# Second merge gate of a hybrid layer: seven block products in place of eight, with x's block sums kept in DRAM

## The chip, the cores and the metric

One Trainium2 chip, one of its cores. The metric is device time in microseconds for one call of the whole layer, as the median over runs. The engines are TensorE (PE in the profile, its weight loads PEld), VectorE (DVE), ScalarE (ACT), GpSimd (POOL) and SyncE (SP), which here only issues DMAs. Each engine works through its own instructions strictly in the order in which they were written into its queue.

## The reference, cut to what matters

One layer on 512 tokens of width 1024, in float32: gated linear attention (GLA), forgetting attention (FoX), a merge of the two by gates, an output projection, then a gated MLP.

```python
h = rmsnorm(x, norm_mix_g)
gq, gk, gv, gr, glr, fq, fk, fv, ff, g_gla, g_fox = jnp.split(h @ w_in, IN_OFFSETS, axis=-1)
o_gla = ...                       # GLA, then norm and silu(gr)
o_fox = ...                       # FoX attention
y = jax.nn.sigmoid(g_gla + gate_b[0]) * (o_gla @ w_gla_branch) \
    + jax.nn.sigmoid(g_fox + gate_b[1]) * (o_fox @ w_fox_branch)
x = x + y @ w_out
a, val = jnp.split(rmsnorm(x, norm_ffn_g) @ w_up, 2, axis=-1)
...
```

The change concerns `g_fox`, the second gate: a product of h (512 x 1024) with a weight of 1024 x 1024.

## The kernel before, in words

**Splits.** Every weight comes from DRAM as a *piece* of 128 x 1024 floats (512 KB). To keep float32 accuracy a piece is split into a high half `wh` (a cast on ACT, L292) and a low half `wl` (raw minus high, on DVE, L293), and `mm3` (L326) issues three matmuls for one product: high by high, high by low, low by high. `wh` and `wl` have three buffers each (NW = 3), so the split of a piece can only begin when PE is done with the piece three places earlier. The raw pieces sit in places named `raw`, `rawz`, `zr`, with two buffers each. A list, `recipes`, fixes the order of the pieces; `behind(n, ...)` hangs loads and adds onto the split of piece n.

**Seven for eight.** Several products are already done in blocks by Strassen's scheme in Winograd's form: the operands are cut into 2 x 2 blocks, sums of blocks are multiplied, and seven block products (numbered 1 to 7) give the four result blocks. The sums of weight blocks are made by DMA: an accumulating transfer on GpSimd's queue adds a block from DRAM onto a raw piece that lies in SBUF. An "add" (L300) does so in place, once the piece has been split and is no longer wanted; a "sum" (`dma_behind`, L306, issued at L310) does so ahead, behind a one-column copy named `tick`. K of FoX, V of FoX, the output projection and both MLP products work like this, and their products with shared pieces stand several pieces apart. `wsum` are sums of blocks of the last weight, made in DRAM in the same way and spread over the kernel by the tables COPY_AT and ADD_AT.

**The stage around the change.** After the attention (whose last matmuls are at L1041) the kernel runs a loop over `c` from -2 to 7 (L1141). One pass makes one tile of the second gate, `gate_tile` (L926: 24 matmuls of 128 x 512, evicted at L933), two passes ahead of its use, and then the two branch products for the 128 features of c (24 matmuls of 128 x 512), two sigmoids (L1127), and the products of gates and branches (L1156, L1157, L1160), whose results are split again for the output projection (L1119, L1120). At the head of this stage ACT and DVE also make the second operand of the branches: `zr` times its sigmoid `sg` on GpSimd (L1132), times `ogr` on DVE (L1133), split to `ogh` (ACT, L1136) and `ogl` (DVE, L1138).

**x's block sums.** In the GLA stage `pair_sums` and `pair_split` (L724, L726) make four sums of blocks of x, split into halves, for FoX's K and V. Their buffers are given up before the attention.

Of the kernel before, what the change touches and what calls it, by code (L numbers as in the profile page):

```python
# [92 lines left out]
def hybrid_kernel(ctx: ExitStack, tc, xT, xt, wp, wu, wd, wf, wn, pp, aw2, fing, out):  # L93
# [232 lines left out]
    def mm3(ps, ah, al, bh, bl, start, stop, **k):  # L326
        mm(ps, lhsT=ah, rhs=bh, start=start, stop=False, **k)  # L327
        mm(ps, lhsT=ah, rhs=bl, start=False, stop=False, **k)  # L328
        mm(ps, lhsT=al, rhs=bh, start=False, stop=stop, **k)  # L329

# [383 lines left out]
    def pair_split(p, after, tag, tag_low=None):  # L714

        hi = gpool.tile([P, K2, H], F32R, tag=tag, name="h" + tag)
        if tag_low is not None:
            lo = gpool.tile([P, K2, H], F32R, tag=tag_low, name="l" + tag_low)
        else:
            if not lows_left:  # L720
                lows = gpool.tile([P, K2, T], F32R, tag="x2", name="lx2")
                lows_left.extend(lows[:, :, i * H : (i + 1) * H] for i in range(2))
            lo = lows_left.pop()
        nc.scalar.copy(out=hi, in_=sources[p])  # L724
        with tc.issue_after(after.ins):
            nc.vector.tensor_sub(out=lo, in0=sources[p], in1=hi.bitcast(F32))  # L726
# [402 lines left out]
    for h in range(GH):  # L1129
# [8 lines left out]
        nc.vector.tensor_sub(out=ogl[h], in0=zr[h], in1=ogh[h].bitcast(F32))  # L1138
# [581 lines left out]
def _layout(inputs):  # L1720
# [21 lines left out]
    for c in range(-GAHEAD, KD):
        if c + GAHEAD < KD:
            ps.append(by_feature(cols("gf", D), c + GAHEAD))
        if c < 0:
            continue
# [69 lines left out]
```

## Time and profile before

| | us |
|---|---|
| median of 3 runs (689.93 to 690.96) | 690.02 |
| the profiled execution | 689.94 |
| its span, first to last instruction | 688.2 |
| PE busy | 681.4 (99%) |
| DVE busy | 547.8 (80%) |
| ACT busy | 431.5 (63%) |
| POOL busy | 135.5 (20%) |

A group's busy time is the union of its instructions' time; a matmul's duration is longer than its share of the array, since matmuls overlap. So the time of a run of matmuls is read from start to start. Rows of the timeline give start, duration, engine, line, operation, output and inputs, and how often. "[2.43 <-POOL zr L1132]" at a row's end says that the engine sat idle for 2.43 us before it and that the instruction on line 1132 ended this.

### The profile page before, as it was taken

Reading aid. Unit: us, or ns where it says so; the run is one execution under the profiler, and the core shown is the slowest. Engines: PE = TensorE matmul, PEld = TensorE weight load, DVE = VectorE, ACT = ScalarE, POOL = GpSimd, SP = SyncE. Lnnn points to the kernel's source line nnn. Section 1 sums busy time; section 2 is a strip of 40 time slices with the busy share of each in tenths; the row PEclk is TensorE's granted clock in tenths of the full one; section 3 lists DMA queues with packets and bytes.
Section 4 is the critical chain, followed back from the end, with each engine's and each line's share of the span. In section 5 each row is a group of like instructions: output and inputs, shape, how many; then the busy total and the mean of one; then the engine's idle time right before and its main releaser. Section 6 shows DMA issues by size and latency. Waiting matters only on the chain.

```text
span 688.2 us, 10637 instructions
## 1 busy us (share of the span) xinstructions
PE 681.4 (99%) x3875; PEld 585.0 (85%) x3875; DVE 547.8 (80%) x856; ACT 431.5 (63%) x698; POOL 135.5 (20%) x196
## 2 busy tenths in 40 slices
PE   9999999999999999999999999999999999999996
PEld 6788888888888888888888999999999999888885
DVE  6774988858776766687689999888899879977884
ACT  7487675677777744344584965665666666655663
POOL 1125110122321424331110112121122111000222
PEclk9999999999999999999999999999999999999999
DMA  8769488998665489968974898999899888865643
GB/s 313 269 190 317 87 274 218 302 218 207 174 150 122 112 248 196 278 152 212 235 235 126 160 221 198 223 225 218 191 215 216 200 202 261 265 203 173 197 139 122
DMA packets 46184, 142.23 MB, mean 207 GB/s; under 512 B 5396, under 2 KB 9388, under 8 KB 46004
## 3 DMA queue, kind: packets, MB, share of 16 engines
q1 hardware_dynamic: 31156, 92.98, 39.8%
q0 software_dynamic: 11808, 43.52, 35.6%
q10 hardware_dynamic: 3168, 5.05, 2.1%
q8 instruction: 30, 0.49, 0.3%
q14 instruction: 22, 0.18, 0.1%
HBM read 137.32 MB, written 27.28 MB: 239 GB/s over the span
## 4 chain that ended last, share of the span: by engine, by line
PE 99%; DVE 1%; issue 0%; ACT 0%; DVEq 0%; ACTq 0%
PE ps_mm L327 20%; PE ps_mm L329 20%; PE ps_mm L328 20%; PE ps_wide L1462 9%; PE ps_wide L327 5%; PE ps_wide L329 5%; PE ps_wide L328 5%; PE ps_wide L1463 4%; PE ps_lg L1041 1%; PE ps_lg L982 1%; PE ps_pt L1016 1%; PE ps_mm L489 1%; PE ps_ax L327 1%; PE ps_ax L328 1%; PE ps_ax L329 1%; PE ps_ax L377 1%
## 5 line engine op out<-in xcount | busy, mean ns | idle before, releaser
L292 ACT CAST wh<-rawx 128x1024 fp32r<-128x1024 f32 x75 | 76.2, 1016 | 57.3 <-PE ps_mm L328 18.1
L327 PE MATMUL ps_mm<-xw,wh 128*128 128x512 f32 (+1 forms) x320 | 109.3, 341 | 0.0
L328 PE MATMUL ps_mm<-xw,wh 128*128 128x512 f32 (+1 forms) x320 | 107.8, 337 | 0.0
L329 PE MATMUL ps_mm<-xw,wl 128*128 128x512 f32 (+1 forms) x320 | 107.7, 337 | 0.0
L293 DVE TENSOR_TENSOR wl<-rawx,wh 128x1024 fp32r<-128x1024 f32 x75 | 88.3, 1178 | 12.4 <-ACT wh L292 11.4
L293 DVE TENSOR_TENSOR wl<-raw,wh 128x1024 fp32r<-128x1024 f32 x58 | 74.6, 1287 | 14.1 <-ACT wh L292 13.9
L292 ACT CAST wh<-raw 128x1024 fp32r<-128x1024 f32 x58 | 60.7, 1049 | 36.0 <-PE ps_mm L328 18.7
L1462 PE MATMUL ps_wide<-xo,wh 128*128 128x512 f32 x192 | 68.6, 399 | 0.0
L327 PEld LDWEIGHTS ps_mm<-xw,wh 128*128 128x128 f32 x320 | 60.5, 189 | 8.3 <-issue 0.9
L329 PEld LDWEIGHTS ps_mm<-xw,wl 128*128 128x128 f32 x320 | 60.5, 189 | 6.6 <-DVE wl L293 0.2
L328 PEld LDWEIGHTS ps_mm<-xw,wh 128*128 128x128 f32 x320 | 60.6, 189 | 5.9 <-DVE xw L1251 0.2
L1463 PE MATMUL ps_wide<-xo,wl 128*128 128x256 f32 x192 | 54.1, 282 | 0.1
L293 DVE TENSOR_TENSOR wl<-rawz,wh 128x1024 fp32r<-128x1024 f32 x31 | 39.2, 1266 | 16.8 <-ACT wh L292 16.6
L300 POOL DMA_DIRECT2D rawx<-in_wu_dram x30 | 26.3, 877 | 115.7 <-DVE wl L293 77.0
L327 PE MATMUL ps_mm<-xc,wh 128*128 128x256 f32 (+1 forms) x136 | 45.0, 331 | 0.0
L328 PE MATMUL ps_mm<-xc,wh 128*128 128x256 f32 (+1 forms) x136 | 44.6, 328 | 0.0
L329 PE MATMUL ps_mm<-xc,wl 128*128 128x256 f32 (+1 forms) x136 | 44.5, 327 | 0.0
L1462 PEld LDWEIGHTS ps_wide<-xo,wh 128*128 128x128 f32 x192 | 36.1, 188 | 8.2
L292 ACT CAST wh<-rawz 128x1024 fp32r<-128x1024 f32 x31 | 32.4, 1045 | 13.6 <-issue 5.0
L327 PE MATMUL ps_mm<-wh,xw 128*128 128x512 f32 x96 | 37.7, 393 | 0.0
L328 PE MATMUL ps_mm<-wl,xw 128*128 128x512 f32 x96 | 37.4, 390 | 0.0
L329 PE MATMUL ps_mm<-wh,xw 128*128 128x512 f32 x96 | 37.4, 389 | 0.0
(492 smaller groups left out, 1796.0 us busy)
## 6 DMA issues: line engine op xcount, KB each, us to landing
rawx<-in_wu_dram POOLq DMA_DIRECT2D x40, 512.0 KB, 6.9
rawz<-in_wp_dram SPq DMA_DIRECT2D x30, 512.0 KB, 5.0
raw<-in_wp_dram SPq DMA_DIRECT2D x22, 512.0 KB, 5.1
wsum<-in_wd_dram SPq DMA_DIRECT2D x20, 512.0 KB, 6.2
rawx<-in_wu_dram SPq DMA_DIRECT2D x20, 512.0 KB, 5.0
raw<-in_wu_dram SPq DMA_DIRECT2D x20, 512.0 KB, 5.1
rawx<-wsum SPq DMA_DIRECT2D x12, 512.0 KB, 3.7
wsum<-in_wd_dram POOLq DMA_DIRECT2D x10, 512.0 KB, 8.6
```

What stands on the lines that cost most here:

```text
L292: nc.scalar.copy(out=hi[:, :m], in_=raw[:, :m])
L293: nc.vector.tensor_sub(out=lo[:, :m], in0=raw[:, :m], in1=hi[:, :m].bitcast(F32))
L300: nc.gpsimd.dma_start(raw, recipes[i][0], accum_op=ALU.add)
L327: mm(ps, lhsT=ah, rhs=bh, start=start, stop=False, **k)
L328: mm(ps, lhsT=ah, rhs=bl, start=False, stop=False, **k)
L329: mm(ps, lhsT=al, rhs=bh, start=False, stop=stop, **k)
L377: mm(warm, lhsT=nc.const_aps.tensor(1.0, (P, P), BF16), rhs=nc.const_aps.tensor(1.0, (P, T), BF16), start=True, stop=True,)
L489: mm(first[i], lhsT=w[:, i * P : (i + 1) * P], rhs=x, start=(k == j == 0), stop=False)
L982: last = mm(lg[:, place_of_q(qb)], lhsT=a[r, q], rhs=b[r, :n], start=(j == 0), stop=(j == 2))
L1016: nc.tensor.transpose(pt[:, i * P : (i + 1) * P], pr[:, c : c + P], ident)
L1462: mm(ps[:, i], lhsT=wh[:, c], rhs=both[p][:, k], start=first and k == 0, stop=False, skip_group_check=True)
L1463: mm(ps[:, i, 0], lhsT=wl[:, c], rhs=both[p][:, k, 0], start=False, stop=k == KH - 1, skip_group_check=True,)
```

## The change

The second gate's eight tiles become two groups of seven block products. A block product takes one piece, and has 2 x 4 x 3 = 24 matmuls of 256 columns in place of 24 of 512. Group 0 runs ahead of all branch tiles; group 1's first product stands between branches 0 and 1, its other six between branches 1 and 2. Within a group the order is 1, 5, 2, 3, 6, 7, 4. One bank of PSUM takes products 1 and 2, one takes 5 and then 3 on top, and a third starts from a copy of product 1 and takes 6, 7 and 4 on top, so that this bank is read out between 6 and 7 and between 7 and 4, and the copies of 1 and 5 are taken before 2 and 3 go on top.

The four sums of blocks of x, high and low halves, are written to DRAM tiles `again` in the GLA stage (8 transfers of 512 KB on SP's queue) and read back when the attention's buffers are free (8 more on the same queue). Six pieces more are split than before (14 for 8). Block sums of the weight are made by one sum and three adds per group: 6 out of 5, 7 out of 3, 4 out of 6. Of the 24 adds of `wsum`, 16 in place of 10 now hang on the splits of the twelve pieces ahead of the second gate, and 8 in place of 14 on later ones.

```diff
-GAHEAD = 2
-ADD_AT = [32 + i if i < 10 else 42 + (i - 10) * 20 // 14 for i in range(24)]
+ADD_AT = [32 + i if i < 4 else 36 + (i - 4) // 2 if i < 16 else 50 + (i - 16) * 4 for i in range(24)]
+GATE_ORDER = (1, 5, 2, 3, 6, 7, 4)
+GATE_PLACE = {(0, 1): "rawz", (0, 5): "rawz", (0, 2): "raw", (0, 3): "raw"}
+GATE_PLACE.update({(1, 1): "raw", (1, 5): "zr", (1, 2): "rawz", (1, 3): "zr"})
+def branch_order():
+    order = [(0, p) for p in GATE_ORDER] + [0, (1, GATE_ORDER[0]), 1] + [(1, p) for p in GATE_ORDER[1:]]
+    return order + list(range(2, KD))
...
+            g, p = what
+            g11, g12, g21, g22 = (wps[n_gate + 2 * q + g] for q in range(4))
+            new, before = {
+                1: (g11, None), 2: (g21, None), 3: (g22, None), 7: (g12, 3), 5: (g12, None), 6: (g22, 5), 4: (g21, 6),
+            }[p]
...
+    for g in range(2):
+        for p, q in ((5, 6), (3, 7), (6, 4)):
+            behind(at_gate[g, p], "add", at_gate[g, q])
+    behind(at_gate[0, 1] - 2, "sum", at_gate[0, 5], at_gate[0, 1])
+    behind(at_gate[0, 4], "load", at_gate[1, 5])
+    behind(at_branch[0], "sum", at_gate[1, 5], at_gate[1, 1])
...
+    again = {p: [dpool.tile([P, KD // 2, H], F32, name=f"again{p}{i}") for i in range(2)] for p in (5, 3, 6, 7)}
...
         pair_ops[p] = (hi, lo)
+        for i, x in enumerate((hi, lo)):
+            nc.sync.dma_start(again[p][i], x.bitcast(F32))
...
+    lows = held_place[:, : KD * T].rearrange("p (a k t) -> p a k t", k=K2, t=H)
+    highs = [later[2][0]] + [x[:, :, t] for x in later[3] for t in (slice(0, H), slice(H, T))]
+    gate_ops = {p: (highs[i], lows[:, i]) for i, p in enumerate((5, 3, 7, 6))}
+    for i in (1, 0):
+        for p in (5, 3, 7, 6):
+            nc.sync.dma_start(gate_ops[p][i].bitcast(F32), again[p][i])
...
+    def gate_product(g, p):
+        name = {1: "x", 2: "x", 5: "z", 3: "z", 6: "y", 7: "y", 4: "y"}[p]
+        first = (g, name) not in gate_banks
+        if first:
+            gate_banks[g, name] = ax_banks[(2, 3)[g] if name == "x" else g]
+        ps = gate_banks[g, name]
+        wh, wl = piece()
+        for i in range(2):
+            for k in range(K2):
+                c = slice((i * K2 + k) * P, (i * K2 + k + 1) * P)
+                with tc.issue_after(last_gate[0].ins) if last_gate else ExitStack():
+                    now = mm3(
+                        ps[:, i * H : (i + 1) * H], wh[:, c], wl[:, c], *gate_operand(p, k), first and i == k == 0,
+                        k == K2 - 1, skip_group_check=True,
+                    )
+        last_gate[:] = [now]
+        t = slice(H, T) if p in (7, 4) else slice(0, H)
+        scale = rb[:, t].unsqueeze(1).broadcast_to([P, 2, H])
+        if p == 1:
+            gate_banks[g, "y"] = pmm()
+            nc.scalar.copy(out=gate_banks[g, "y"], in_=ps)
+        elif p in (5, 3):
+            nc.scalar.copy(out=pairs(left[:, 2 + p // 5]), in_=pairs(ps))
+        elif p in (6, 7):
+            z = z_pair(g, 1)[:, :, t]
+            minus_sum(z, pairs(ps), pairs(left[:, p - 4]))
+            nc.vector.tensor_mul(out=z, in0=z, in1=scale)
+        else:
+            nc.vector.tensor_mul(out=z_pair(g, 0)[:, :, t], in0=pairs(ps), in1=scale)
...
-    for c in range(-GAHEAD, KD):
-        if c + GAHEAD < KD:
-            zf[c + GAHEAD] = bpool.tile([P, T], F32, tag="zf", name="zf", bufs=GAHEAD + 1)
-            for _ in gate_tile(zf[c + GAHEAD]):
-                pass
-        if c < 0:
+    for c in branch_order():
+        if not isinstance(c, int):
+            gate_product(*c)
             continue
```

What this makes of the queues shows at three places. Lines of the changed kernel have numbers of their own: there L314 and L315 are the two halves of a split, L322 an add, L330 and L332 the tick and the transfer behind it, L1190 and L1192 the copies out of PSUM, L1207 the difference taken from PSUM (`minus_sum`), L1211 the sigmoids, L1216, L1217, L1220 and L1222 the making of `ogh` and `ogl`.

The first place is ACT at the head of the stage. Before:

```order
L1127 ACTIVATE sg_2628<-zr_1382 128x512
L1127 ACTIVATE sg_2635<-zr_1383 128x512
L1127 ACTIVATE sg_2642<-zr_1383 128x512
L1136 CAST ogh0_2608<-zr_1382 128x512
L1136 CAST ogh1_2609<-zr_1382 128x512
L1136 CAST ogh2_2610<-zr_1383 128x512
L292 CAST wh_2686<-raw_2350 128x1024
L1136 CAST ogh3_2611<-zr_1383 128x512
```

And now, with `ps_ax_2652` the bank of products 5 and 3, `wh_2714` the piece of product 3, `wh_2746`, `wh_2778`, `wh_2809` those of 6, 7, 4:

```order
L1211 ACTIVATE sg_2663<-zr_1398 128x512
L1190 COPY ps_mm_2712<-ps_ax_2654 128x512
L1211 ACTIVATE sg_2670<-zr_1399 128x512
L1220 CAST ogh0_2631<-zr_1398 128x512
L1220 CAST ogh1_2632<-zr_1398 128x512
L1211 ACTIVATE sg_2677<-zr_1399 128x512
L314 CAST wh_2714<-raw_2380 128x1024
L1220 CAST ogh2_2633<-zr_1399 128x512
L1220 CAST ogh3_2634<-zr_1399 128x512
L314 CAST wh_2746<-rawz_2178 128x1024
L1192 COPY left_2643<-ps_ax_2652 128x512
L314 CAST wh_2778<-raw_2380 128x1024
```

The fourth sigmoid has moved behind the second `ogh`, and the copy of product 5 stands behind all four `ogh` and the splits of pieces 3 and 6.

The second place is DVE right after it. Before, the gate tiles' evictions and the splits take turns:

```order
L293 TENSOR_TENSOR wl_2687<-raw_2350,wh_2686 128x1024
L1138 TENSOR_TENSOR ogl3_2647<-zr_1383,ogh3_2611 128x512
L933 TENSOR_TENSOR zf_2684<-ps_mm_2685,rb_104 128x512
L293 TENSOR_TENSOR wl_2720<-rawz_2476,wh_2719 128x1024
L933 TENSOR_TENSOR zf_2717<-ps_mm_2718,rb_104 128x512
L293 TENSOR_TENSOR wl_2753<-rawz_2522,wh_2752 128x1024
```

And now, `ps_mm_2712` being the bank of products 6, 7 and 4 of group 0:

```order
L1217 SCALAR_TENSOR_TENSOR zr_1399<-ogr2_117,ppt_92,zr_1399 128x512
L1217 SCALAR_TENSOR_TENSOR zr_1399<-ogr3_118,ppt_92,zr_1399 128x512
L315 TENSOR_TENSOR wl_2715<-raw_2380,wh_2714 128x1024
L1222 TENSOR_TENSOR ogl2_2675<-zr_1399,ogh2_2633 128x512
L1222 TENSOR_TENSOR ogl3_2682<-zr_1399,ogh3_2634 128x512
L315 TENSOR_TENSOR wl_2747<-rawz_2178,wh_2746 128x1024
L1198 TENSOR_TENSOR left_2643<-ps_ax_2654,rb_104 128x2x256
L315 TENSOR_TENSOR wl_2779<-raw_2380,wh_2778 128x1024
L315 TENSOR_TENSOR wl_2810<-rawz_2178,wh_2809 128x1024
L1207 SCALAR_TENSOR_TENSOR zf_2839<-ps_mm_2712,left_2643 128x2x256
L1196 TENSOR_TENSOR zf_2839<-zf_2839,rb_104 128x2x256
L315 TENSOR_TENSOR wl_2843<-rawz_2719,wh_2842 128x1024
```

The read-out of product 6 (the first L1207 row) now stands behind the splits of pieces 7 and 4 (`wl_2779`, `wl_2810`).

The third place is GpSimd, at the head of the stage. Before:

```order
L1132 TENSOR_TENSOR zr_1382<-zr_1382,sg_2621 128x512
L1132 TENSOR_TENSOR zr_1382<-zr_1382,sg_2628 128x512
L1132 TENSOR_TENSOR zr_1383<-zr_1383,sg_2635 128x512
L1132 TENSOR_TENSOR zr_1383<-zr_1383,sg_2642 128x512
L308 COPY tick_90<-wl_2720 128x1
L310 DMA wsum1_70<-wsum0_69 128x1024
```

And now, with `rawz_2178` the raw piece of products 5, 6 and 4 and `raw_2380` that of 3 and 7:

```order
L322 DMA rawz_2178<-in_wp_dram 128x1024
L1216 TENSOR_TENSOR zr_1398<-zr_1398,sg_2656 128x512
L1216 TENSOR_TENSOR zr_1398<-zr_1398,sg_2663 128x512
L1216 TENSOR_TENSOR zr_1399<-zr_1399,sg_2670 128x512
L1216 TENSOR_TENSOR zr_1399<-zr_1399,sg_2677 128x512
L322 DMA raw_2380<-in_wp_dram 128x1024
L322 DMA rawz_2178<-in_wp_dram 128x1024
L330 COPY tick_90<-wl_2843 128x1
L332 DMA zr_2813<-in_wp_dram 128x1024
```

The adds that turn piece 3 into 7 and piece 6 into 4 stand directly behind the four products `zr`. On PE, 24 matmuls of product 6 are followed at once by the 24 of product 7; between 7 and 4 stand four matmuls of branch 0 (in group 1 four of branch 2).

More of the change, by code (lines that the diff above doesn't have):

```diff
@@ L167, in fresh @@
         rotation += 1
-    at_branch = {}
-    for i, w in enumerate(wps[16:n_out]):
+    at_branch, at_gate = {}, {}
+    for w in wps[16 : 16 + GH + KD]:
         fresh(w)
-        c = c_of_piece(i - GH - KD)
-        if c is not None:
-            at_branch[c] = len(recipes) - 1
-            if c in HELD:
-                at_out[1, HELD.index(c)] = len(recipes)
-                fresh(o11[HELD.index(c)])
+    n_gate = 16 + GH + KD
+    for what in branch_order():
+        if isinstance(what, int):
+            c = what
+            at_branch[c] = len(recipes)
+            recipes.append((wps[n_gate + 8 + c], None, 1024, C_PLACE[c]))
+            if c in HELD:
+                r = HELD.index(c)
+                at_out[1, r] = len(recipes)
+                recipes.append((o11[r], None, 1024, HELD_PLACE[r]))
+        else:
[4 more added lines that the diff above has]
+            }[p]
+            at_gate[g, p] = len(recipes)
+            recipes.append((new, at_gate[g, before] if before else None, 1024, GATE_PLACE.get((g, p))))
     for p in OUT[1:]:
@@ L328, in mm3 @@
         mm(ps, lhsT=ah, rhs=bl, start=False, stop=False, **k)
[L329 removed]
+        return mm(ps, lhsT=al, rhs=bh, start=False, stop=stop, **k)
     def feature_tile(ps, w, xh, xl, w0=0, nk=KD, m=P):
@@ L1110, in operand @@
         ts = [bpool.tile([P, KD // 2, m], F32R, name=f"o{c}{n}") for c in halves]
+        later.append(ts)
         return [[t[:, k] for k in range(KD // 2)] for t in ts]
-    o1, o7, o3, o65, o24 = operand(1), operand(7), operand(3), operand(65, T), operand(24, T, "h")
-    o24.append([])
-    oops = {1: (o1, 0), 7: (o7, 0), 3: (o3, 0), 6: (o65, 0), 5: (o65, H), 2: (o24, 0), 4: (o24, H)}
+    later = []
+    o1, o7, o3, o65 = operand(1), operand(7), operand(3), operand(65, T)
+    left = bpool.tile([P, KD // 2, T], F32, tag="oh24", name="left")
@@ new lines, in pairs, with z_pair @@
+    def pairs(ps):
+        return ps.rearrange("p (i t) -> p i t", t=H)
+    gate_banks, z_of, last_gate = {}, {}, []
+    ax_banks = [pax() for _ in range(4)]
+    def z_pair(g, right):
+        if (g, right) not in z_of:
+            z_of[g, right] = bpool.tile([P, 2, T], F32, tag="zf", name="zf", bufs=2) if right else left[:, :2]
+        return z_of[g, right]
+    def gate_product(g, p):
[25 more added lines that the diff above has]
+            nc.vector.tensor_mul(out=z, in0=z, in1=scale)
+        else:
+            nc.vector.tensor_mul(out=z_pair(g, 0)[:, :, t], in0=pairs(ps), in1=scale)
@@ L1166, in hybrid_kernel @@
             k = c - KD // 2
+            if k == 0:
+                high24 = bpool.tile([P, KD // 2, T], F32R, tag="oh24", name="oh24")
+                o24 = [[high24[:, i] for i in range(KD // 2)], []]
+                oops.update({2: (o24, 0), 4: (o24, H)})
             nc.gpsimd.tensor_add(out=z, in0=z, in1=zg[c])
@@ L1741, in _layout @@
     ps += [by_feature(cols("gg", D), c) for c in range(KD)]
[L1742 to L1746, printed above, removed]
+    gf = cols("gf", D).reshape(2, KD // 2, P, 2, 2, 2, P).transpose(0, 3, 4, 2, 5, 1, 6)
+    ps += list(gf.reshape(8, P, 1024))
+    for c in range(KD):
         ps.append(
```

25 lines of the change are left out of this document (14 added, 11 removed).

## The prediction

> **What bounds the kernel now.** I read the page first, then the chain of waits, then the stretch that the change rewrites.
>
> ```profile
> PE 681.4 (99%) x3875; PEld 585.0 (85%) x3875; DVE 547.8 (80%) x856; ACT 431.5 (63%) x698; POOL 135.5 (20%) x196
> PE 99%; DVE 1%; issue 0%; ACT 0%; DVEq 0%; ACTq 0%
> ```
>
> PE is busy 99% of the span and the chain is 99% PE: time is saved by shorter matmul work and lost by every wait of PE. The stretch runs from the attention's last matmul to the output projection's first (table by stretch, then the timeline of PE at its two ends, then a stretch of 256-column products from the MLP):
>
> ```profile
> core 0: us, PE busy (x) PEld busy (x) DVE busy (x) ACT busy (x) POOL busy (x), PEclk, DMA share, GB/s
> 224.88:312.00 87.12, 87.12 (x386) 72.13 (x386) 60.66 (x77) 39.00 (x56) 32.61 (x41) 1.00 0.79 195
> 224.88 0.45 PE L327 MATMUL ps_mm<-xw,wh 128*128 128x512 f32 x1
> 312.00 0.39 PE L327 MATMUL ps_mm<-held,oh 128*128 128x512 f32 x1
> 442.61 0.28 PE L1463 MATMUL ps_wide<-xw,wl 128*128 128x256 f32 x1
> 445.60 0.40 PE L1462 MATMUL ps_wide<-xo,wh 128*128 128x512 f32 x1
> ```
>
> PE never stops here: 87.12 us for 384 matmuls of 512 columns, 0.2269 each. Between the last two rows lie 24 matmuls of 256 columns, with L1463 itself 25: 2.99/25 = 0.12 us each. DVE has 60.7 and ACT 39.0 us of work in the stretch.
>
> **What is removed and added on PE.** 192 x 0.2269 = 43.5 us go, 14 x 24 x 0.12 = 40.3 come: a gain of 3.2 us if PE never waits. A block product lasts 2.88 us where a gate tile lasted 5.44, so each split, read-out and add has half the time. Added to ACT are 6 casts and 6 copies from PSUM, to DVE 6 subtractions and 4 more evictions; prices, by operation:
>
> ```profile
> L292 ACT CAST wh<-rawz x7: 1035/1047/1053, 240.6 to 295.7; 128x1024 fp32r<-128x1024 f32 x7
> L293 DVE TENSOR_TENSOR wl<-rawz,wh x7: 1215/1217/2243, 242.2 to 297.1; 128x1024 fp32r<-128x1024 f32 x7
> L1264 ACT COPY ox<-ps_mm x2: 587/592/597, 319.4 to 319.9; 128x512 f32<-128x512 f32 x2
> L1123 DVE SCALAR_TENSOR_TENSOR ap<-ps_mm,joint x10: 683/686/691, 394.5 to 480.0; 128x512 f32<-128x512 f32 x10
> L1160 POOL TENSOR_TENSOR zg<-zf,zg x4: 1288/1290/2200, 247.7 to 280.3; 128x512 f32<-128x512 f32 x4
> ```
>
> That is 6 x 1.05 + 6 x 0.59 = 9.8 us for ACT and 6 x 1.22 + 4 x 0.69 = 10.1 for DVE: room on average, so the sum goes by four waits. I follow them with the clock of the trace, where product 1 of group 0 starts at 224.88.
>
> **Wait 1, the operands from DRAM.** SP's queue issues the high halves behind the load of the piece for group 1's product 1, which waits until the piece of product 2 is split:
>
> ```profile
> 223.57 1.23 DVE L293 TENSOR_TENSOR wl<-raw,wh 128x1024 fp32r<-128x1024 f32 x1 [0.28 <-ACT wh L292]
> 224.83 0.33 SPq L263 DMA_DIRECT2D raw<-in_wp_dram  x1
> rawz<-in_wp_dram SPq DMA_DIRECT2D x30, 512.0 KB, 5.0
> DMA to landing us min/median/max: 3.1/3.1/3.1
> ```
>
> So the high half for product 5 is issued at about 225.2 and lands 3.1 (one lone load at 238.03) to 5.0 us later (median of 30); I take the middle, 229.3. Product 5 was due at 227.8: +1.5, and products 5 and 2 end at 235.1.
>
> **Wait 2, the copy of product 5.** Product 3 adds onto product 5's bank, so the copy on ACT comes first, and that stands behind all of `ogh`. Before, that chain ran so:
>
> ```profile
> 229.57 1.14 ACT L1127 ACTIVATE sg<-zr 128x512 f32<-128x512 f32 x2
> 231.58 0.63 ACT L1127 ACTIVATE sg<-zr 128x512 f32<-128x512 f32 x1 [0.88 <-POOL zr L1132]
> 235.09 0.62 ACT L1136 CAST ogh<-zr 128x512 fp32r<-128x512 f32 x1 [1.08 <-DVE zr L1133]
> 237.31 1.05 ACT L292 CAST wh<-raw 128x1024 fp32r<-128x1024 f32 x1
> 230.26 5.94 POOL L1132 TENSOR_TENSOR zr<-zr,sg 128x512 f32<-128x512 f32 x4 [4.11 <-ACT sg L1127]
> 231.59 5.17 DVE L1133 SCALAR_TENSOR_TENSOR zr<-ogr,ppt,zr 128x512 f32<-128x512 f32 x3 [2.43 <-POOL zr L1132]
> 236.68 1.89 DVE L1138 TENSOR_TENSOR ogl<-zr,ogh 128x512 fp32r<-128x512 f32 x3
> 238.48 0.74 DVE L1133 SCALAR_TENSOR_TENSOR zr<-ogr,ppt,zr 128x512 f32<-128x512 f32 x1
> ```
>
> The gate tiles covered it; a DVE step costs 1.72 us while POOL multiplies (5.17/3) and 0.74 alone. In the new order the second `ogh` ends as before at 235.7, and only then comes the fourth sigmoid (236.3) and its product on POOL (1.29, to 237.6). DVE does two `ogl` (to 236.3), the third step under POOL (238.1), the fourth (238.8), `wl` of piece 3 (240.0), two `ogl` (241.3), `wl` of 6 (242.5). ACT's fourth `ogh` waits for the fourth step (239.4), then come the cast of 6 (240.5) and the copy (241.1). Product 3 starts there, not at 235.1: +6.0. It ends at 244.0, product 6 at 246.9.
>
> **Wait 3, two adds ahead of the read-out of product 6.** Product 7 writes the bank that holds 6, so the read-out comes first, which DVE holds behind the splits of 7 and 4; piece 4 is an add onto piece 6. Adds land so (lines of the adds and of the sums between 205 and 360 us):
>
> ```profile
> L300 POOL DMA_DIRECT2D zr<-in_wp_dram x4: 863/876/902, 304.8 to 334.7; - x4
> DMA to landing us min/median/max: 5.5/7.2/9.8
> L310 POOL DMA_DIRECT2D wsum<-wsum x12: 777/818/1189, 225.4 to 305.7; - x12
> DMA to landing us min/median/max: 5.8/8.6/11.3
> ```
>
> Add 7 follows 240.0, add 4 follows 242.5 and lands 7.2 later (the adds' median), 249.8; cast 250.9, `wl` 252.1, read-out 252.8. Product 7 starts at 252.9 instead of 246.9: +6.0. It ends at 255.8; four matmuls of branch 0 (0.9) cover its own read-out, +0.1, and product 4 ends at 259.7.
>
> The Trainium skill, "DMA: Bandwidth & Descriptors", section "Anatomy of one DMA — SWDGE (gpsimd) path", fits such a DMA as 2.0 us plus bytes over 436 GB/s, here 3.2 us for 512 KB. By it add 4 would land at 245.7, product 7 would start at 248.7, and with group 1 likewise the estimate would be some 9 us lower than mine. The trace disagrees: no add lands in under 5.5.
>
> **Wait 4, the same in group 1.** Branch 0 ends at 264.2. Product 5's first three matmuls stand ahead of branch 1, and its `wl` is made while POOL adds zg (2.24 instead of 1.22, the maximum in the L293 row): +0.4. Branch 1 ends at 273.2 and product 5 at 275.8, product 6 at 284.4. Its `wl` is made at 278.3, behind zg's sum on POOL and the small halves of branch 1:
>
> ```profile
> 249.02 0.41 ACT L1119 CAST oh<-zg 128x256 fp32r<-128x256 f32 x1 [1.23 <-POOL zg L1160]
> 249.99 0.41 DVE L1120 TENSOR_TENSOR ol<-zg,oh 128x256 fp32r<-128x256 f32 x1
> ```
>
> Add 4 follows on POOL at 278.5, behind add 7 and one `wsum` add. With three in flight I take the sums' median, 8.6, so 287.1; cast, split and read-out end at 290.1. Product 7 was due at 284.4: +5.8, and +0.1 behind it.
>
> **What costs nothing.** The eight stores of x's sums follow on SP's queue when their low halves are made, the last here:
>
> ```profile
> 83.03 1.22 DVE L726 TENSOR_TENSOR lx<-x,hfgs 128x1024 fp32r<-128x1024 f32 x1
> 86.64 0.33 SPq L263 DMA_DIRECT2D rawz<-in_wp_dram  x1
> ```
>
> At 84.3 two stores are left; the queue's next load goes at 86.64 anyway. The low halves' loads go after the last use of V, before anything needs them. The `wsum` adds, moved, add 0 to 1 us: ahead of the attention's masks on POOL, or between adds of the output projection; I take 0. Everything else on ACT and DVE lies beside the waits counted.
>
> **Sum.** -3.2 + 1.5 + 6.0 + 6.0 + 0.1 + 0.4 + 5.8 + 0.1 = +16.7 us. Against the profiled execution (span 688.2, time 689.94) that is 706.6; the median of the runs is 0.08 higher: 706.7.
>
> **Bounds.** Adds at their fastest (5.5 in group 0, 5.8 in group 1) take 1.7 and 2.8 off; operands after 3.1 us take nothing, since wait 2 swallows it; without the slowing by POOL, wait 2 is 1.5 shorter: 700.7. Adds at their slowest (9.8 and 11.3) add 2.6 and 2.7: 712.0.
>
> **Rivals.**
>
> *PE's clock falls in the gaps.* Three gaps of about 6 us open where PE never stopped before. The only cold PE here is the kernel's start:
>
> ```profile
> 0.85 4.42 PE L377 MATMUL ps_ax<-const-bfloat16-1.0 128*128 128x512 bf16 x10 [0.85 <-PEq L1803]
> ```
>
> Ten matmuls of 512 columns took 4.42 us there, where 2.27 is the warm price: 2.15 lost. If each gap costs that once, 3 x 2.15 = 6.5 more: 713. The Trainium skill, "TensorE: Matmul & The Clock Gate", Part 1, says just that: half rate after an idle window of some 3.4 us, until a busy window has passed. No gap of that length stands inside the trace of before.
>
> *The waits are half as long.* If the read-outs find their splits done earlier (adds in 5.5 us and less queueing on ACT than I lay out), waits 2, 3 and 4 shrink by half, 9 us: 698. For it: on average ACT would have 49 us of work in 84 and DVE 71. Against it: the order of the queues is fixed.
>
> *Faster.* The adds land in time, PE never stops, and only the 3.2 us count: 686.8. The mechanism is the chain from `wl` of 6 through add 4, cast, split and read-out to product 7. Its split can begin when product 5 ends and gives back its buffers, so at best that `wl` is ready 3.4 us ahead of product 6; with that product's 2.88 this leaves 6.3 us, of which cast, split and read-out take 3.0: the add must land in 3.3 us for no wait, and under about 4.9 for two waits to stay below 3.2. No add does (5.5).
>
> **Chances.** The forecast 0.60, the cold clock 0.20, half waits 0.10, faster 0.06, no change 0.04. Slower by over 0.2% is thus 0.90, within 0.2% (about what a measurement here can tell from nothing, 1.4 us) 0.04, faster 0.06. The range from 697 to 715 takes in the first three cases and leaves out the last two and the tails.
>
> **What would show it.** PE's idle time between 225 and 315, near 0 before, should be about 20 us: ahead of the first matmuls of products 3 and 7, ended by ACT's copy out of `ps_ax` and by DVE's `minus_sum` (L1207). Block products should run at 2.88 us; ACT's casts of pieces 7 and 4 should wait for the adds. A granted clock below 1.00 behind the gaps would speak for the first rival. I am wrong if product 7 follows 6 within some 2 us.

## The result, and the profile after

The changed kernel takes 717.29 us (median of 4 runs, 717.03 to 719.23) against 689.97 (689.78 to 690.96): 27.3 us more, a ratio of 1.040 (95% interval 1.0378 to 1.042). The forecast was 706.7 with a range from 697 to 715: the direction held, the size did not. The profiled execution is the slowest of the four (719.23, span 717.5).

The page's first line and its chain, of the changed kernel, as shown of the kernel before:

```profile
PE 688.5 (96%) x4019; PEld 595.9 (83%) x4019; DVE 556.7 (78%) x866; ACT 440.5 (61%) x710; POOL 145.8 (20%) x206
PE 74%; DMA 10%; issue 6%; DVE 5%; ACT 3%; POOL 1%; DVEq 0%; ACTq 0%; POOLq 0%
```

PE was 99% of the chain; now a quarter of it is transfers, other engines and time in which an engine waited for nothing that the profile shows ("issue"). PE is also busy 7 us longer, though it has 3.2 us less to do. The same stretch as in the prediction, from the attention's end to the output projection's first matmul (table by stretch), and the waits of PE (total, times, longest):

```profile
225.60:334.47 108.87, 91.34 (x530) 82.33 (x530) 69.42 (x85) 47.74 (x68) 31.03 (x34) 0.92 0.73 186
```
```profile
PE ps_mm L349 <- issue: 6.7, 1, 6.7
PE ps_mm L349 <- DVE zf L1207: 5.4, 1, 5.4
PE ps_mm L349 <- DVE x2t L1291: 3.0, 1, 3.0
PE ps_ax L349 <- DMA oh<-again: 2.9, 1, 2.9
PE ps_ax L349 <- ACT left L1192: 1.3, 1, 1.3
PE ps_ax L349 <- DVE oo L1078: 1.1, 1, 1.1
```

The stretch lasts 108.9 us where it lasted 87.1. PE stands still for 17.5 of them, and the granted clock (the column after the five engines) is 0.92 on average, where it was 1.00. Of the waits, the third lies in the output projection, outside this stretch. When the others end (timeline of PE, with the idle time ahead of each row):

```profile
225.49 0.27 PE L1066 MATMUL ps_lg<-pl,v 128*128 128x128 f32 x1
226.81 0.39 PE L349 MATMUL ps_ax<-xw,wh 128*128 128x256 f32 x1 [1.05 <-DVE oo L1078]
232.87 0.39 PE L349 MATMUL ps_ax<-oh,wh 128*128 128x256 f32 x1 [2.92 <-DMA oh<-again]
241.62 0.38 PE L349 MATMUL ps_ax<-oh,wh 128*128 128x256 f32 x1 [1.25 <-ACT left L1192]
254.30 0.55 PE L349 MATMUL ps_mm<-oh,wh 128*128 128x256 f32 x1 [6.66 <-issue]
293.37 0.58 PE L349 MATMUL ps_mm<-oh,wh 128*128 128x256 f32 x1 [5.44 <-DVE zf L1207]
```

These are the attention's last matmul (it stood at 224.77) and products 1, 5, 3 and 7 of group 0 and 7 of group 1. The forecast had 241.1 for product 3 and 252.9 for product 7. For the gap of 6.66 the profile names no releaser; the read-out of product 6 ends right ahead of the row at 254.30, behind the split of piece 4 (timeline of DVE):

```profile
252.37 1.23 DVE L315 TENSOR_TENSOR wl<-rawz,wh 128x1024 fp32r<-128x1024 f32 x1 [2.21 <-ACT wh L314]
253.51 0.68 DVE L1207 SCALAR_TENSOR_TENSOR zf<-ps_mm,left 128x512 f32<-128x512 f32 x1
```

The clock around the second gap (table by stretch), and matmuls of 256 columns right behind it:

```profile
247.00:250.00 3.00, 0.64 (x6) 0.43 (x4) 1.07 (x1) 1.53 (x2) 0.00 (x0) 1.00 1.05 225
250.00:253.00 3.00, 0.00 (x0) 0.00 (x0) 0.79 (x2) 1.71 (x2) 0.00 (x0) 0.73 0.52 178
253.00:256.00 3.00, 1.70 (x8) 1.73 (x9) 2.96 (x4) 0.28 (x1) 0.00 (x0) 0.50 0.44 137
256.00:259.00 3.00, 3.00 (x19) 3.00 (x19) 0.06 (x1) 0.00 (x0) 1.04 (x2) 0.63 0.69 227
```
```profile
254.86 0.41 PE L351 MATMUL ps_mm<-oh,wl 128*128 128x256 f32 x1
255.07 0.41 PE L349 MATMUL ps_mm<-oh,wh 128*128 128x256 f32 x1
```

The clock falls to 0.50 within the gap and stays there until about 258.3: these matmuls start 0.21 us apart, not 0.12. Summed over each cold stretch, starts against the warm price, this costs 1.6 us behind the gap of 2.92, 1.8 behind 6.66, 2.7 behind 5.44 and 1.7 behind 2.97: 7.8 us.

Where the time went, in three parts (the output projection's and the MLP's first matmul; 312.00 was shown before):

```profile
334.47 0.39 PE L349 MATMUL ps_mm<-held,oh 128*128 128x512 f32 x1
380.86 0.39 PE L349 MATMUL ps_mm<-xw,wh 128*128 128x512 f32 x1
```
```profile
352.76 0.39 PE L327 MATMUL ps_mm<-xw,wh 128*128 128x512 f32 x1
```

| | before | after | change | forecast |
|---|---|---|---|---|
| up to the output projection | 312.0 | 334.5 | +22.5 | +16.7 |
| output projection | 40.8 | 46.4 | +5.6 | 0 |
| the rest of the span | 335.4 | 336.6 | +1.2 | 0 |

These rows are of the profiled execution, so they add up to 29.3 us and not to the 27.3 of the medians. The second row came as a surprise. GpSimd there (timeline), what ACT waits for, and how long the output projection's adds take to land, in this kernel and, last, in the one before:

```profile
349.95 0.88 POOL L322 DMA_DIRECT2D rawz<-in_wp_dram  x1 [10.40 <-DVE wl L315]
350.53 0.89 POOL L330 COPY tick<-wl 128x1 f32<-128x1 f32 x1
351.37 0.83 POOL L332 DMA_DIRECT2D wsum<-wsum  x1
351.91 1.21 POOL L322 DMA_DIRECT2D rawz<-in_wp_dram  x1
```
```profile
363.43 1.04 ACT L314 CAST wh<-rawz 128x1024 fp32r<-128x1024 f32 x1 [5.10 <-DMA rawz<-in_wp_dram]
```
```profile
DMA to landing us min/median/max: 6.3/11.7/12.7
```
```profile
DMA to landing us min/median/max: 6.0/8.3/9.8
```

A `wsum` add now stands between two adds of the output projection's own pieces. The second of these lands after 11 us, its cast is late, and PE waits 3.0 us and then runs cold.

### The profile page after: what moved, and what is told of

Its sections match the earlier page's. It is cut to its first block, busy times and chain, and to the rows that moved or that the text cites. A ratio compares the mean times of both kernels' runs of the same rounds, so it can differ in the third digit from the quotient of the medians.

```text
span 717.5 us, 11001 instructions
## 1 busy us (share of the span) xinstructions
PE 688.5 (96%) x4019; PEld 595.9 (83%) x4019; DVE 556.7 (78%) x866; ACT 440.5 (61%) x710; POOL 145.8 (20%) x206
## 4 chain that ended last, share of the span: by engine, by line
PE 74%; DMA 10%; issue 6%; DVE 5%; ACT 3%; POOL 1%; DVEq 0%; ACTq 0%; POOLq 0%
PE ps_mm L349 14%; PE ps_mm L350 14%; PE ps_mm L351 14%; PE ps_wide L1546 8%; PE ps_wide L1547 4%; DMA cb<-nct 4%; PE ps_wide L350 4%; PE ps_wide L349 4%; PE ps_wide L351 4%; DMA rawz<-in_wp_dram 3%; DVE wl L315 2%; ACT wh L314 1%; DMA zr<-in_wp_dram 1%; DMA rawx<-in_wu_dram 1%; PE ps_lg L1007 1%
## 5 line engine op out<-in xcount | busy, mean ns | idle before, releaser
L314 ACT CAST wh<-rawx 128x1024 fp32r<-128x1024 f32 x75 | 76.2, 1016 | 57.4 <-PE ps_mm L350 20.8
L315 DVE TENSOR_TENSOR wl<-rawx,wh 128x1024 fp32r<-128x1024 f32 x75 | 88.2, 1176 | 12.4 <-ACT wh L314 12.3
L349 PE MATMUL ps_mm<-xw,wh 128*128 128x256 f32 (+1 forms) x280 | 92.9, 332 | 0.0
L314 ACT CAST wh<-raw 128x1024 fp32r<-128x1024 f32 x59 | 61.7, 1048 | 49.1 <-PE ps_mm L350 23.4
L350 PE MATMUL ps_mm<-xw,wh 128*128 128x256 f32 (+1 forms) x280 | 91.4, 326 | 0.0
L351 PE MATMUL ps_mm<-xw,wl 128*128 128x256 f32 (+1 forms) x280 | 91.3, 326 | 0.0
L315 DVE TENSOR_TENSOR wl<-raw,wh 128x1024 fp32r<-128x1024 f32 x59 | 74.8, 1269 | 18.4 <-ACT wh L314 18.2
L349 PEld LDWEIGHTS ps_mm<-xw,wh 128*128 128x128 f32 x280 | 53.0, 189 | 6.8 <-issue 0.9
L315 DVE TENSOR_TENSOR wl<-rawz,wh 128x1024 fp32r<-128x1024 f32 x31 | 39.2, 1265 | 23.1 <-ACT wh L314 22.7
L351 PEld LDWEIGHTS ps_mm<-xw,wl 128*128 128x128 f32 x280 | 53.1, 189 | 4.8 <-DVE wl L315 0.3
L350 PEld LDWEIGHTS ps_mm<-xw,wh 128*128 128x128 f32 x280 | 53.1, 190 | 4.1 <-DVE xw L1335 0.2
L322 POOL DMA_DIRECT2D rawx<-in_wu_dram x30 | 26.4, 880 | 116.9 <-DVE wl L315 70.4
L330 POOL COPY tick<-wl 128x1 f32<-128x1 f32 x39 | 18.6, 478 | 127.4 <-DVE wl L315 127.4
L314 ACT CAST wh<-rawz 128x1024 fp32r<-128x1024 f32 x31 | 32.3, 1045 | 15.1 <-DMA rawz<-in_wp_dram 7.0
L349 PE MATMUL ps_mm<-xc,wh 128*128 128x256 f32 (+1 forms) x128 | 41.1, 321 | 0.0
L350 PE MATMUL ps_mm<-xc,wh 128*128 128x256 f32 (+1 forms) x128 | 40.6, 317 | 0.0
L351 PE MATMUL ps_mm<-xc,wl 128*128 128x256 f32 (+1 forms) x128 | 40.5, 317 | 0.0
L349 PE MATMUL ps_mm<-wh,xw 128*128 128x512 f32 x96 | 37.7, 393 | 0.0
```

The lines of the kernel that those rows point to most:

```text
L314: nc.scalar.copy(out=hi[:, :m], in_=raw[:, :m])
L315: nc.vector.tensor_sub(out=lo[:, :m], in0=raw[:, :m], in1=hi[:, :m].bitcast(F32))
L322: nc.gpsimd.dma_start(raw, recipes[i][0], accum_op=ALU.add)
L330: now = nc.gpsimd.tensor_copy(out=tick, in_=lo[:, 0:1].bitcast(F32))
L351: return mm(ps, lhsT=al, rhs=bh, start=False, stop=stop, **k)
```

## Experiments

Each stands beside runs of the kernel before on the same chip (689.97 to 690.35 us); ratios are to these. The intervals of e1_adds_out, e2_warm, e3_read6 and e8_resident overlap that of the changed kernel (1.0378 to 1.042), so that their totals alone decide little; there the argument goes by the traces.

### The output projection's adds

**e1_adds_out**

```diff
-... else 50 + (i - 16) * 4 for i in range(24)]
+... else 50 + (i - 16) * 4 if i < 21 else 80 + 2 * (i - 21) for i in range(24)]
```

> The last three adds of wsum move from the splits 70, 74 and 78 (the first two in the output projection) to 80, 82 and 84 (the MLP's first pieces); nothing else changes. Theory: the new waits of 0.50 and 2.97 us in the output projection, and the half-clock matmuls behind the longer one (about 4 us of them, 2 us lost), come from a wsum add that runs between the adds of the output projection's own pieces. Then both waits go: 717.3 falls to 711.5-713.5. Rival: these waits come from the stretch being later or from other traffic; then 716.5-718.

716.71 us, ratio 1.0385 (1.0365 to 1.0404): a miss in the total and a hit in the place. The output projection took 41.6 us, its wait of 3.0 is gone; but from the MLP's start, where the adds now stand, the span lasts 3.3 us longer than in the changed kernel (340.0 against 336.6), with new waits of which these are two:

```profile
PE ps_wide L1547 <- DVE wl L315: 1.2, 1, 1.2
PE ps_mm L349 <- ACT wh L314: 1.2, 1, 1.2
```

**e5_adds_early**

```diff
-ADD_AT = [32 + i if i < 4 else 36 + (i - 4) // 2 if i < 16 else 50 + (i - 16) * 4 for i in range(24)]
+ADD_AT = [32 + i if i < 4 else 36 + (i - 4) // 2 for i in range(16)] + [50, 54, 58, 60, 61, 63, 64, 66]
```

> Of the changed kernel only the last eight wsum adds move: from the splits 50, 54, 58, 62, 66, 70, 74, 78 to 50, 54, 58, 60, 61, 63, 64, 66, so that none but the last (as in the kernel before) stands among the output projection's adds, and none in the MLP, where e1_adds_out had put three of them and given its gain of 5 us back. Theory (the collision of transfers is what the output projection lost): it takes 41-42 us again in place of 46.4, nothing new waits in the MLP: 711-713. Rival (the wsum adds need this room wherever they stand; the branch tiles lose what the output projection gains): 715-718.

714.00 us, 1.0336 (1.0319 to 1.0354): 3.3 us of the loss lay in the place of these last eight adds. In the profile the output projection takes 42.7 us and the rest 335.9; one wait of 0.9 is left. The total is 1 us over what was expected.

### The clock

**e2_warm**

```diff
+FILL = {6: 22}
...
         last_gate[:] = [now]
+        if p in FILL:
+            with tc.issue_after(last_gate[0].ins):
+                for _ in range(FILL[p]):
+                    now = mm(
+                        ax_banks[(3, 0)[g]], lhsT=nc.const_aps.tensor(1.0, (P, P), BF16),
+                        rhs=nc.const_aps.tensor(1.0, (P, T), BF16), start=True, stop=True, skip_group_check=True,
+                    )
+            last_gate[:] = [now]
```

> After product 6 of each group PE gets 22 matmuls of constants (128x512 bf16, 5.0 us at the warm price of 0.227) that nothing reads; the waits stay. Clock theory: with PE busy in the gaps of 6.7 and 5.4 us the granted clock stays at 1.00, products 7 and 4 run at 0.12 us per matmul of 256 columns in place of 0.21, and the 4.1 us of half clock behind the first gap and the 5.5 behind the second give back 2.0 and 2.7: 711.8-713.5, with the starts of product 7 where they were. Rival (the products are slow there for another reason, such as operands or weights just written, and the lower clock is only a sign of idle time): 716.5-718, or slower if the fillers delay product 7.

714.31 us, 1.0355 (1.0325 to 1.0384): 3.0 less, where 3.8 to 5.5 were expected. The mechanism shows in the traces. Product 7 of group 0 starts at 254.30 in both, by chance to the hundredth (in e2_warm the read-out of product 6 had ended at 253.6, and the fillers held product 7 for 0.7 us more, which is part of what the total missed); the same work then follows, 24 matmuls of product 7 and four of branch 0. Its first row and the first of the branch in e2_warm, and the branch's first in the changed kernel (timeline of PE):

```profile
254.30 0.47 PE L350 MATMUL ps_mm<-oh,wh 128*128 128x256 f32 x1
257.37 0.40 PE L350 MATMUL ps_mm<-ogh,wh 128*128 128x512 f32 x1
```
```profile
258.96 0.40 PE L349 MATMUL ps_mm<-ogh,wh 128*128 128x512 f32 x1
```

The branch begins at 257.37 with the fillers and at 258.96 without, 1.6 us later. In group 1 product 7 takes 3.0 us with them (292.40 to 295.38) and 5.3 without (293.37 to 298.66). So PE's own idleness makes the products slow, not their operands.

**e9_both**: the edit of e5_adds_early, and fillers at four places:

```diff
+FILL = {(0, 1): 9, (0, 2): 5, (0, 6): 20, (1, 6): 20}
```

> The changed kernel with both things that the forecast had left out taken away: the last wsum adds placed as in e5_adds_early, and matmuls of constants in all four gaps of the second gate (9 after product 1 and 5 after product 2 of group 0, 20 after product 6 of each group). The waits for copies, adds and read-outs, of which the forecast's sum was made, all stay. Theory (the forecast missed because of the clock and of the output projection's adds, and its sum of waits was about right): 705-709, around the forecast of 706.7. Rival (the waits themselves were mis-sized, or the fillers' gains do not add up): 710-714.

712.60 us, 1.0316 (1.029 to 1.0341), which is the rival's time. But the four executions fall apart: 709.43 at a clock of 1.000, and 711.94 to 713.28 at 0.991 to 0.993. Only the first was profiled.

**e12_full**: fillers long enough to leave next to nothing of the gaps.

```diff
-FILL = {(0, 1): 9, (0, 2): 5, (0, 6): 20, (1, 6): 20}
+FILL = {(0, 1): 14, (0, 2): 7, (0, 6): 27, (1, 6): 25}
```

> As e9_both with longer fillers: 14, 7, 27 and 25 matmuls of constants in place of 9, 5, 20 and 20, so that nearly nothing is left of the gaps (in e9_both's profile 1.7, 0.8, 2.4 and 1.7 us were left). e9_both had a clock of 1.000 and 709.4 us in one execution and 0.991 to 0.993 with 712 to 713.3 in three. Theory (what was left of the gaps, 1.7-2.4 us, still let the clock fall in those three): all executions at 0.998 or more and 708-711 (a filler may delay a product by some tenths). Rival (the clock falls elsewhere, in the output projection or the MLP): 0.991-0.994 and 712-714 again.

708.82 us, 1.0268 (1.0254 to 1.0282), as expected, and all five executions lie between 708.07 and 709.23. The clock, and what is left of PE's waits in the gate (the longest and the one for the read-out of product 6):

```profile
core 0: 707.1 us, clock 0.998
```
```profile
PE ps_ax L350 <- DVE oo L1079: 1.1, 1, 1.1
PE ps_mm L350 <- DVE zf L1216: 0.2, 1, 0.2
```

The fillers take no wait away, they only keep the clock. Against e5_adds_early that is worth 5.2 us. The forecast's sum of waits is thereby measured by itself: 708.82 - 690.08 = 18.7 us, where it said 16.7.

### The waits

**e3_read6**

```diff
-        wh, wl = piece()
+        with tc.issue_after(read6[g].ins) if p == 7 else ExitStack():
+            wh, wl = piece(2 if p == 6 else NW)
```

(`read6` holds the read-out of product 6.)

> On DVE the read-out of product 6 now stands ahead of the split of piece 4 (it stays behind that of piece 7); nothing else moves but the same pair in group 1 and one split behind it. Theory (product 7 waits for the split of piece 4, which waits for the second add): product 7 starts right after the split of piece 7 and the read-out, at about 250.9 in place of 254.3, and lies in the gap; the rest of the gap, under 2 us, stands ahead of product 4, so PE also stays warm: 2.9 us and up to 2 of clock per group, 717.3 becomes 708-712. Rival (the read-out is late for another reason, the first add or the copy of product 3): 716-718.

714.95 us (713.24 to 717.49), 1.0366 (1.0335 to 1.0396): 2.3 less, a miss. Product 7 behaves as said in group 0 and not in group 1 (timeline of PE in e3_read6):

```profile
250.12 0.39 PE L349 MATMUL ps_mm<-oh,wh 128*128 128x256 f32 x1 [2.12 <-DVE zf L1210]
289.28 0.58 PE L349 MATMUL ps_mm<-oh,wh 128*128 128x256 f32 x1 [4.73 <-DVE zf L1210]
```

In group 0 it comes 4.2 us earlier, in group 1 the gap shrinks by 0.7 only. What the read-out needs besides the bank is the copy of product 3, and in group 1 ACT has that behind the cast of piece 4 (timelines of ACT and of DVE, changed kernel, and, last, the read-out on DVE in e3_read6):

```profile
290.36 1.04 ACT L314 CAST wh<-zr 128x1024 fp32r<-128x1024 f32 x1 [3.53 <-DMA zr<-in_wp_dram]
291.31 0.58 ACT L1192 COPY left<-ps_ax 128x512 f32<-128x512 f32 x1
```
```profile
291.49 1.23 DVE L315 TENSOR_TENSOR wl<-zr,wh 128x1024 fp32r<-128x1024 f32 x1 [2.27 <-ACT wh L314]
292.63 0.68 DVE L1207 SCALAR_TENSOR_TENSOR zf<-ps_mm,left 128x512 f32<-128x512 f32 x1
```
```profile
288.53 0.69 DVE L1210 SCALAR_TENSOR_TENSOR zf<-ps_mm,left 128x512 f32<-128x512 f32 x1 [2.49 <-ACT left L1193]
```

So in the changed kernel the read-out stands directly behind DVE's split of piece 4 in group 1 too, but the copy on ACT ends at 291.9, only 0.8 us before that split. With the split out of the way (e3_read6) the read-out waits for this copy. Both groups wait for the add of piece 4: group 0 by DVE's queue alone, group 1 by DVE's and by ACT's. The gap of 2.12 still cost 1.7 us of clock.

**e4_plain**: the gate's adds as plain writes; sums of weight blocks are left out.

```diff
-                nc.gpsimd.dma_start(raw, recipes[i][0], accum_op=ALU.add)
+                if i in at_gate.values():
+                    nc.gpsimd.dma_start(raw, recipes[i][0])
+                else:
+                    nc.gpsimd.dma_start(raw, recipes[i][0], accum_op=ALU.add)
```

> The six in-place adds of the second gate become plain writes of the same block on the same queue (the pieces 6, 7 and 4 are then single blocks, not sums). Theory (an accumulating transfer is slow by itself): they land 3-5 us after issue in place of about 8, product 7 starts 3-4 us earlier in each group, and the gaps are short enough that the clock stays: 705-711. Rival (what is slow is the traffic beside them, DMA share 1.0 there): landings as before, 716-718.

712.74 us, 1.0332 (1.0306 to 1.0358). Landings between 235 and 300 us, of the changed kernel's adds and of these writes:

```profile
DMA to landing us min/median/max: 5.4/6.9/8.0
```
```profile
DMA to landing us min/median/max: 3.6/4.0/6.0
```

The accumulating transfer is some 2 to 3 us slower than a plain one on the same queue, as the theory had it, and product 7 follows product 3 after 9.75 us in place of 12.68. (Ahead of product 3 stood 4.1 us in this profile, where the changed kernel had 1.25; so only the distance between the two products is compared.) The gaps of 2.2 and 3.5 us that remain cooled PE all the same (1.6 and 2.5 us lost); the total is 1.7 us over the expected range. The Trainium skill's fit for such a transfer ("DMA: Bandwidth & Descriptors", section "Anatomy of one DMA — SWDGE (gpsimd) path"), by which an estimate for 512 KB is 3.2 us, lies near the faster ones of these plain writes; with adds the trace shows twice that.

**e8_resident**

```diff
-        if p in gate_ops:
-            return tuple(a[:, k] for a in gate_ops[p])
-        i, j = {1: (0, 0), 2: (0, 1), 4: (1, 1)}[p]
+        i, j = {1: (0, 0), 2: (0, 1), 4: (1, 1)}.get(p, (0, 0))
...
-            nc.sync.dma_start(gate_ops[p][i].bitcast(F32), again[p][i])
```

> The changed kernel without the eight loads of x's sums: products 5, 3, 7 and 6 take blocks of x that lie in SBUF, which leaves x's sums out of the result; the order of products and the stores stay. Theory (wait 1 is swallowed by wait 2): product 5 starts at about 229.7 in place of 232.9, but product 3 still starts near 241.5 and the rest as before: 715.5-718. Rival (the loads delay the stage, by themselves or through the traffic that they make for the piece loads and adds): product 3 and all behind it 2-4 us earlier, 712-714.5.

713.44 us (711.84 to 717.97), 1.0346 (1.031 to 1.0383): inconclusive. Product 3 starts at 237.38 in place of 241.62, which is the rival's case; but with the loads gone the order on ACT changed too, and the copy of product 5 now stands ahead of the last two `ogh` and of the cast of piece 6. Product 3 still follows that copy. What the loads cost by themselves stays open.

### Another order of the same work

**e6_order** (the banks and the raw pieces' places change with it, and the tables of e5_adds_early's kind):

```diff
-    order = [(0, p) for p in GATE_ORDER] + [0, (1, GATE_ORDER[0]), 1] + [(1, p) for p in GATE_ORDER[1:]]
-    return order + list(range(2, KD))
+    order = [(0, 1), (1, 1), (0, 5), (0, 2), (0, 3), (0, 6), 0, (0, 7), 1, (0, 4), "0", "1"]
+    order += [(1, 5), (1, 2), (1, 3), (1, 6), 2, (1, 7), 3, (1, 4), "2", "3"]
+    return order + [x for c in range(4, KD) for x in (c, str(c))]
```

A number is a branch's matmuls, a number in quotes its read-out. In this version and the next, part of the sum in the bank of products 6, 7 and 4 is lost, so that their result is not the layer's; the work is the same, and e10_order3 has another bank.

> The same work in another order, with the wsum adds kept out of the output projection and the MLP: both groups' product 1 first, then 5, 2, 3, 6 of group 0, the matmuls of branch 0, product 7, the matmuls of branch 1, product 4, and group 1 likewise with branches 2 and 3; the branches' read-outs follow product 4. Theory (the time went where a dependent product stood with nothing of PE's between it and the add, the split and the read-out): the gaps of 6.7 and 5.4 us and their half clock go; left are 1 us at the stage's head, some 3-4 us ahead of product 3 (the copy of product 5 still stands behind the making of ogh) with 1.8 us of half clock: 690-695. Rival (DMA and DVE cannot feed the block products at this rate in any order): 700-710.

699.53 us, 1.0137 (1.0122 to 1.0152): 14.5 us less than e5_adds_early, with a whole branch between 6 and 7 and between 7 and 4, though not as much as expected. Two waits of 2.1 and 2.3 remain at the head; in the profile 5.0 us are lost up to the output projection (316.96) and 5.1 in it.

**e7_order2**

```diff
+            if c == (0, 5):
+                with tc.issue_after(copy5[0].ins):
+                    og_halves((2, 3))
```

> As e6_order, and the second half of making ogh (h = 2 and 3) is put behind the copy of product 5 on ACT. Theory (wait 2 is only the place of that copy in ACT's queue): product 3 follows product 2 without a wait, PE stays warm: 687-691, against before about 0 or a gain of up to 3. Rival (the late split of piece 3 or the late operands from DRAM keep product 3 back, or branch 0 waits for ogh instead): as e6_order or 1-3 us slower.

698.32 us, 1.0116 (1.0091 to 1.0141), a miss. Up to the output projection it does nearly what was said (312.86, before 312.00). There it loses 4.6 us (timeline of PE):

```profile
322.77 0.50 PE L354 MATMUL ps_mm<-wh,ol 128*128 128x512 f32 x1 [0.28 <-DVE ol L1212]
325.56 0.51 PE L352 MATMUL ps_ax<-wh,oh 128*128 128x512 f32 x1 [0.91 <-ACT wh L317]
326.82 0.74 PE L353 MATMUL ps_ax<-wl,oh 128*128 128x512 f32 x1 [0.76 <-DVE wl L318]
327.36 0.63 PE L354 MATMUL ps_ax<-wh,ol 128*128 128x512 f32 x1
```

Three short waits in 4 us, none over 0.91, and PE runs cold to 330.

**e10_order3** and **e11_order4** went on from there. The first's edit against e7_order2, without the other banks that move along:

```diff
-            gate_banks[g, "y"] = ax_banks[2 - g]
+            gate_banks[g, "y"] = pmm()
...
-            nc.gpsimd.tensor_add(out=z, in0=z, in1=zg[c])
+            nc.vector.tensor_add(out=z, in0=z, in1=zg[c])
```

> As e7_order2, with two edits: the bank that takes products 6, 7 and 4 is one of the other four PSUM banks, since in e6_order and e7_order2 part of the sum in that bank was lost (their results differ from the reference, their work does not); and in the last four branches the sum of the two gated products is made on DVE (0.69 us) in place of GpSimd (2.2 us there, with DVE's own instructions slowed beside it). Theory (what e7_order2 lost in the output projection, 4.6 us between its first matmul and the first transposes, comes from DVE running late at the end of the branches: three waits of 0.3, 0.9 and 0.8 us within 5 us, and 1.7 us of half clock behind them): the waits and the half clock go, 692-695. Rival (the output projection waits for its pieces or for DMA): 696-699 as e7_order2. To beat the kernel before it would have to come under 689, which no theory here expects.

And e11_order4 against e10_order3:

```diff
-ADD_AT = [32 + i if i < 4 else 36 + (i - 4) // 2 for i in range(16)] + [56, 58, 60, 61, 62, 63, 64, 66]
+ADD_AT = [32 + i if i < 4 else 36 + (i - 4) // 2 for i in range(16)] + [50, 51, 53, 56, 58, 60, 61, 63]
...
-    behind(at_branch[0], "load", at_gate[1, 5])
-    behind(at_gate[0, 7], "sum", at_gate[1, 5], at_gate[1, 1])
+    behind(at_gate[0, 3], "load", at_gate[1, 5])
+    behind(at_branch[0], "sum", at_gate[1, 5], at_gate[1, 1])
...
-            gate_banks[g, name] = ax_banks[g if name == "x" else 2]
+            gate_banks[g, name] = ax_banks[2] if name == "z" else ax_banks[1] if g else pmm()
```

> As e10_order3, with three edits: product 5 of group 1 takes its raw piece in the buffer that comes free first (its sum was issued 9 us before its cast there, and product 5 waited 1.0 and 0.8 us with 1.9 us of half clock behind); product 1 of group 0 takes a PSUM bank that the attention does not use (1.05 us); the last eight wsum adds stand earlier, out of the full stretch at the end of the branches, where the residual's loads came late (1.6 us ahead of the output projection's second product). Theory (these three are what is left of e10_order3's 5.4 us over the kernel before): 690-692, within 0.3% of the kernel before and not faster, since splits, copies and read-outs of 14 pieces for 8 leave DVE little slack. Rival (each wait removed opens the next): 694-696. Third way: under 688.5, the saved matmul work showing at last.

They took 695.73 us, 1.0083 (1.0067 to 1.01), and 695.77, 1.0085 (1.0071 to 1.0099). The first is 0.7 over what was expected: in its profile the output projection takes 42.7 us in place of 45.4, but 3.9 are lost ahead of it. The second is its rival's case: the output projection takes 40.8 us, as before the change, but 4.9 are lost ahead of it; the waits that were removed are gone, and others stand in their place (waits of PE in e11_order4):

```profile
PE ps_ax L352 <- ACT wh L317: 2.0, 1, 2.0
PE ps_mm L354 <- DVE wl L318: 1.5, 2, 1.3
PE ps_ax L352 <- ACT left L1200: 0.6, 1, 0.6
```

No version tried beats the kernel before.

## Why the prediction was wrong

By the runs the 27.3 us are 18.7 of waits less the saved matmuls, 5.2 of clock and 3.3 of the moved `wsum` adds (717.29, less 3.29 by e5_adds_early, less 5.18 by e12_full; the 3.3 hold what the clock cost in the output projection). The forecast's 16.7 was a sum of the first kind alone.

- **PE's work** was right: block products take 2.88 us when warm (279.13, 282.01 and 284.89 are starts of three in a row).
- **Wait 1** was undersized. The high half was issued at 226.0, near the 225.2 forecast, and product 5 began 6.9 us later, where I took the middle of 3.1 and 5.0. The DMA engines were full there (share 1.03 between 226 and 229 us), and the load used as the lower bound was a lone one. It mattered little: product 3 came at 241.6 for 241.1, so that wait 2 swallowed it as the bounds said.
- **Wait 2** was right to 0.5 us, **wait 3** to 1.4 (254.30 for 252.9; add 4 was issued at 243.3, not 242.5, and landed after 8.0 us, not 7.2). **Wait 4** was right in size (5.44 for 5.8) and in its path: the read-out stands directly behind DVE's split of piece 4. What the forecast did not see is the second path, ACT's copy of product 3, which was ready only 0.8 us before; so taking the first away brought 0.7.
- **The clock** is the larger failing step: the sum has no term for it, and it cost 5.2. The rival was sized well, 2.15 us a gap against 1.6 to 2.7 measured, 1.9 on average (its 4.42 us run to the end of the tenth matmul; from start to start the ten take 4.07, since the next starts at 4.92, and 1.8 are lost). But it stood as an alternative with 0.20, though nothing in the profile spoke against it once the forecast itself had opened gaps of 6 us. It belonged in the sum: 706.7 + 6.5 = 713. In the changed kernel it did not come where the rival had its first gap, since only 1.25 us were left ahead of product 3. It came behind product 1 instead, where wait 2 swallowed it, and at a gap in the output projection.
- **"What costs nothing"** held the other failing step. I allowed the moved `wsum` adds 0 to 1 us, "between adds of the output projection", and took 0; there they cost 3.3. Their landing time was in the prediction (8.6 us), and so was that of the adds beside them (7.2), but the sum let more than one in flight land later in wait 4 alone, and not here.
- The 2.0 us that are left over the forecast lie, by e12_full's profile, at three places: 0.7 up to product 3 (241.81 for 241.1; the attention ended 0.9 later, and ACT's chain with it), 0.4 more up to product 7 of group 0, and 0.8 in the output projection (41.6 us for 40.8). Product 1 also waited 1.05 us for a bank that the attention still held, which the forecast did not name; wait 2 swallowed it.

The bounds of 700.7 to 712.0 spanned the adds' landing times and POOL's slowing of DVE; neither failing step was in them.

## What to carry to other kernels

Where a change makes PE wait in a place in which it never waited, price the wait and the cold stretch behind it together, and count the small waits that follow one another. A block scheme needs other work between products that depend on each other through an add, a split and a read-out: here an order with a whole branch tile in each such place (and the banks and tables that go with it) brought back 14 us. When transfers are moved to other pieces, look up what else is in flight at each new place.

## What the runs showed of the hardware

- The granted clock fell behind shorter gaps than expected: 2.12, 2.24, 2.92 and 2.97 us each cost 1.6 to 1.7, one of 1.80 ahead of product 3 in e5_adds_early 1.5, and in e7_order2 three waits of 0.28, 0.91 and 0.76 within 4 us did it too; single gaps of 1.05, 1.25 and 1.60 (e10_order3) did not, nor did one of 2.35 behind fillers (e9_both). The Trainium skill ("TensorE: Matmul & The Clock Gate", Part 1) names an idle window of about 3.4 us that runs freely; several gaps here are shorter than that, and why they suffice was not tested.
- PE kept busy with matmuls that nobody reads made a kernel faster (714.00 to 708.82). Steadier it was only where the fillers cover nearly the whole of the gaps: the executions of e12_full spread over 1.2 us, those of e2_warm over 4.7 and of e9_both over 3.9 (e5_adds_early, without fillers, 1.9), with four or five executions each.
